# The down stage of an FFN with ScalarE and VectorE in written order: loads of forms three products early, weight sums a unit early

## The chip, the cores and the metric

The kernel runs on one core of one Trainium2 chip. Its engines are TensorE (PE in the profile, its weight loads PEld), VectorE (DVE), ScalarE (ACT), GpSimd (POOL) and SyncE (SP), which issues most of the transfers. The metric is the device time of one execution in microseconds. Each engine works off its own list of instructions in order; semaphores make one engine wait for another.

## The reference

One decoder layer over 512 tokens with 2048 features, float32 in and out. A mixing part (a gated linear recurrence beside RWKV heads) ends in a projection `w_o` with a residual; then comes the feed-forward part that this case is about:

```python
def ffn(h):                       # D_MODEL 2048, D_FF 6144, 512 tokens
    u = rmsnorm(h, ln_ffn)
    g = causal_dwconv(u @ w_gate, conv_f_w, conv_f_b)
    return h + (gelu(g) * (u @ w_up)) @ w_down
```

(in shortened form); after it a gated per-layer embedding and a last norm.

## The kernel before

A float32 product is made from three TensorE products of rounded parts. Each operand is split: ScalarE copies it, rounded, to a high half (`split` L146 for forms of the data, L133 for weights), and VectorE subtracts the high half from the raw value for the low half (L147, L134). Then high times high, high times low and low times high are summed in PSUM (L1382 to L1384 in the down stage, L1274 to L1276 in the gate stage).

Stages that the change touches, in order of time:

- **wo** (L1250 on): for each of 16 feature blocks `m` a product, then VectorE's residual add into `hT[m]` (L1253), then `forms(m)`, which makes from `hT[m]` the block's part of seven operand forms of the next stage (L1241 to L1243, splits L147, L149, L150), then a square for the norm (summed at L1261).
- **gate stage**: gate and up products of the FFN for 48 blocks `n`, each by a Winograd scheme that needs seven units (q5, p1, p4, p6, p7, p2, p3) in place of eight products. A unit takes a weight of 128x1024, which is either loaded as it is or is a sum of quarters of the matrix. `gate_unit` makes these sums, by VectorE (L1127, L1137, L1140) or by an accumulating transfer of GpSimd's queue. `unit` puts the results together; for the last block its closing VectorE addition is L1306 and frees the buffer `e` that it read.
- **down stage**: the hidden features stand in 12 chunks. Chunks 0 to 10 go through a Winograd scheme again, in four groups, seven products for each half `b` of the output:

```python
GROUPS = [(0, 3), (3, 6), (6, 9), (9, 11)]
ORDER = (1, 0, 4, 2, 3, 5, 6)
```

  `down(g, b)` loops over the seven products; each product takes one weight unit of each chunk of its group, and each unit is 12 matmuls of 128x512. The data forms of a group are up to 21 tiles s0 to s20 (tag 3j + chunk within the group, j the product's place in `ORDER`), loaded by the sync queue (L1342) from DRAM and then split; both halves `b` use them, and the next group's forms take the same tiles. Weights of a product 1 or 4 of `ORDER`'s numbers are sums of two quarters by VectorE (`down_unit` L1162, L1168), those of 2 and 6 are accumulated by GpSimd's queue (L1172), 0 and 3 use a quarter that is there, and 5 loads its quarter into one of two buffers `wraw` (L124). A product's result is taken from PSUM by ScalarE in group 0 (L1397) and added by VectorE in the others (L1399). After each half of the last group seven sums (L1407) turn the product sums `PT` into output blocks.
- **the end of the FFN**: `residual`, `down_last` (chunk 11, by plain products of four "last" forms) and `to_features` for four column blocks. `residual` transposes the stored `hT` and adds it (L1427), `down_last` adds its products (L1437).

What sets the order. TensorE's list is in written order. The lists of VectorE, ScalarE and the queues in the stages above are set by a scheduler that simulates the program and takes what is ready by priority; `high_priority(offset=...)` moves an instruction ahead by so many steps. Weights go through a queue: `wqueue` holds the list of all units, and `wnext` hands out the next split unit after `wfill` has prepared ones up to three ahead (`LOOK` 3, and three buffers each of `whi` and `wlo`, so that a unit's high half can be written once TensorE has finished the unit three before). `wfill` makes the raw weight, including its loads and its sum, directly ahead of its split, all with a high priority:

```python
    def wfill(self):
        with self.tc.high_priority(offset=W['offw']):
            self.wfill_()
```

The forms of group g + 1 are loaded and split by one function, called after each product of the half b = 1 of group g; those of group 0 during the units of block 47 of the gate stage.

Of the kernel before, what the change touches and what calls it, by code (L numbers as in the profile page):

```python
# [89 lines left out]
class Builder:  # L90
# [13 lines left out]
    def wqueue(self, items):  # L104
        self.wq = list(items)
        self.wn = 0
        self.wt = []
# [5 lines left out]
    def wfill_(self):  # L113
        nc = self.nc
        while self.wn < len(self.wq) and len(self.wt) < self.LOOK:
            src, shape, *own = self.wq[self.wn]
            self.wn += 1
            if callable(src):
                raw = src()
            elif self.wraw:  # L120
                raw = self.wraw.pop(0)
            else:
                raw = self.t(self.cp, "wraw", shape, bufs=self.RAW)
                nc.sync.dma_start(raw, src)  # L124
# [989 lines left out]
    def gate_unit(self, n, u):  # L1114
# [5 lines left out]
        def load(k, i, j):  # L1120
            t = buf(k)
            nc.sync.dma_start(t, src(i, j))
            return t
        g = self.gw.setdefault(n, {})
        if u == "q5":
            g[21], g[22], g["s"] = load(0, 1, 0), load(1, 1, 1), buf(3)
            nc.vector.tensor_tensor(g["s"], g[21], g[22], ALU.add)  # L1127
            return g["s"]
# [5 lines left out]
        if u == "p7":  # L1134
            if n < 2:
                g[11] = load(2, 0, 0)
            nc.vector.tensor_tensor(g[21], g[21], g[11], ALU.add)  # L1137
            return g[21]
        if u == "p6" and n in (0, NF - 1):
            nc.vector.tensor_tensor(g["s"], g["s"], g[11], ALU.add)  # L1140
        else:
            nc.gpsimd.dma_start(g["s"], src(0, 0 if u == "p6" else 1), accum_op=ALU.add)
# [67 lines left out]
    def phase2(self):  # L1210
# [70 lines left out]
        def unit(n, u):  # L1281
# [29 lines left out]
            if n == NF - 1:  # L1311
                for i in {"q5": (0,), "p1": (1,), "p4": (2, 3), "p6": (4,), "p7": (5,), "p2": (6,)}.get(u, ()):
                    group_form(0, ORDER[i])
# [25 lines left out]
        def hidden(src, tag):  # L1339
            t = T("s%d" % tag, 1, (128, 2, 2, 256), F32R)  # L1340
            r = t[:, 1].bitcast(F32)
            nc.sync.dma_start(r, src)  # L1342
            self.split(t[:, 0], t[:, 1], r)
            return t[:, 0], t[:, 1]

# [5 lines left out]
        def group_form(g, i):  # L1351
            lo, hi = GROUPS[g]
            for ch in range(lo, hi):
# [3 lines left out]
                hids[ch, i] = hidden(src, 3 * ORDER.index(i) + ch - lo)  # L1357
# [28 lines left out]
        def down(g, b):  # L1386
            lo, hi = GROUPS[g]
            for j, i in enumerate(ORDER):
                ps = [self.mm(), self.mm()]
                for ch in range(lo, hi):  # L1390
                    w = self.wnext()
                    for tt in range(2):
                        product(ps[tt], hids[ch, i], w, tt, ch == lo, ch == hi - 1)
# [299 lines left out]
```

## Time and profile before

| | us |
|---|---|
| median of three runs | 2630.39 |
| the three runs | 2632.26, 2629.11, 2630.39 |
| profiled execution | 2625.72 |
| its span (first to last instruction) | 2624.0 |
| mean granted TensorE clock | 0.988 |
| wo to gate | about 902 |
| down stage | about 1883 to 2344 |

The profiled execution is 4.67 us shorter than the median of the runs. In the profile's rows a time in brackets is the idle time of the engine ahead of the instruction, with what ended it. `s<-dd` and `s<-rd` are loads of forms, `x<-wd`, `s<-wd`, `e<-wd` and `wraw<-wd` loads of down weights, numbers of buffers left out. The groups of chunks change at about 1960 to 2040, 2090 to 2165 and 2215 to 2265 us.

### The profile page before, as it was taken

Reading aid. Unit: us, or ns where it says so; the run is one execution under the profiler, and the core shown is the slowest. Engines: PE = TensorE matmul, PEld = TensorE weight load, DVE = VectorE, ACT = ScalarE, POOL = GpSimd, SP = SyncE. Lnnn points to the kernel's source line nnn. Section 1 sums busy time; section 2 is a strip of 40 time slices with the busy share of each in tenths; the row PEclk is TensorE's granted clock in tenths of the full one; section 3 lists DMA queues with packets and bytes.
Section 4 is the critical chain, followed back from the end, with each engine's and each line's share of the span. In section 5 each row is a group of like instructions: output and inputs, shape, how many; then the busy total and the mean of one; then the engine's idle time right before and its main releaser. Section 6 shows DMA issues by size and latency. Waiting matters only on the chain.

```text
span 2624.0 us, 51665 instructions
## 1 busy us (share of the span) xinstructions
PE 2545.0 (97%) x21922; PEld 2241.5 (85%) x21922; DVE 1907.0 (73%) x2603; ACT 1251.5 (48%) x1735; POOL 229.8 (9%) x251
## 2 busy tenths in 40 slices
PE   9989999999999999999999999999999999999997
PEld 8867777777877799999999999999877877787887
DVE  5764875767666978878888888788756777896447
ACT  6563555546433644444444444444545344434335
POOL 0010000101121010000000000000000000000001
PEclk9999999999999999999999999999999999999998
DMA  7222222222343667676677766777767776843223
GB/s 252 93 69 66 87 80 66 86 73 94 94 126 103 222 154 193 177 192 164 191 185 185 188 184 167 193 183 188 220 160 225 189 206 188 233 116 111 96 93 108
DMA packets 131304, 393.76 MB, mean 150 GB/s; under 512 B 14464, under 2 KB 26624, under 8 KB 131072
## 3 DMA queue, kind: packets, MB, share of 16 engines
q1 hardware_dynamic: 111200, 318.10, 35.9%
q0 software_dynamic: 19872, 72.36, 16.7%
q8 instruction: 171, 2.80, 0.4%
q14 instruction: 61, 0.50, 0.1%
HBM read 353.97 MB, written 36.44 MB: 149 GB/s over the span
## 4 chain that ended last, share of the span: by engine, by line
PE 60%; DMA 5%; DVE 4%; ACT 2%; issue 1%; POOL 0%; SPq 0%; POOLq 0%; ACTq 0%; DVEq 0%
PE mm L1275 9%; PE mm L1274 9%; PE mm L1276 9%; PE mm L1383 4%; PE mm L1384 4%; PE mm L1382 4%; PE wk L1274 3%; PE wk L1275 3%; PE wk L1276 3%; PE mm L1488 2%; DMA s<-rd 2%; PE mm L1490 2%; PE mm L1489 2%; DVE wlo L134 2%; PE mm L163 2%; PE mm L165 2%
## 5 line engine op out<-in xcount | busy, mean ns | idle before, releaser
L133 ACT ACTIVATE whi<-x 128x1024 fp32r<-128x1024 f32 x296 | 313.1, 1058 | 410.5 <-PE mm L1275 232.4
L134 DVE TENSOR_TENSOR wlo<-x,whi 128x1024 fp32r<-128x1024 f32 x296 | 361.4, 1222 | 114.0 <-ACT whi L133 107.7
L1274 PE MATMUL mm<-s,whi 128*128 128x256 f32 x1432 | 406.2, 284 | 5.3 <-ACT s L149 4.1
L1275 PE MATMUL mm<-s,whi 128*128 128x256 f32 x1432 | 406.1, 284 | 0.3 <-DVE s L150 0.3
L133 ACT ACTIVATE whi<-wraw 128x1024 fp32r<-128x1024 f32 (+1 forms) x229 | 232.7, 1017 | 363.8 <-PE mm L165 174.3
L1276 PE MATMUL mm<-s,wlo 128*128 128x256 f32 x1432 | 405.9, 283 | 0.0
L134 DVE TENSOR_TENSOR wlo<-wraw,whi 128x1024 fp32r<-128x1024 f32 (+1 forms) x229 | 278.9, 1219 | 157.6 <-ACT whi L133 156.1
L163 PE MATMUL mm<-x,whi 128*128 128x512 f32 x832 | 331.7, 399 | 1.1 <-DVE hT L453 0.9
L167 PE MATMUL mm<-x,wlo 128*128 128x512 f32 x832 | 331.7, 399 | 0.0
L165 PE MATMUL mm<-x,whi 128*128 128x512 f32 x832 | 330.3, 397 | 0.0
L1382 PE MATMUL mm<-whi,s 128*128 128x512 f32 x680 | 269.6, 398 | 14.7 <-ACT whi L133 14.6
L1383 PE MATMUL mm<-wlo,s 128*128 128x512 f32 x680 | 271.3, 399 | 10.6 <-DVE wlo L134 10.0
L1274 PEld LDWEIGHTS mm<-s,whi 128*128 128x128 f32 x1432 | 275.5, 192 | 5.8 <-ACT s L149 4.3
L1275 PEld LDWEIGHTS mm<-s,whi 128*128 128x128 f32 x1432 | 275.6, 192 | 0.6 <-DVE s L150 0.6
L1276 PEld LDWEIGHTS mm<-s,wlo 128*128 128x128 f32 x1432 | 275.6, 192 | 0.0
L1384 PE MATMUL mm<-whi,s 128*128 128x512 f32 x680 | 268.7, 395 | 0.0
L163 PEld LDWEIGHTS mm<-x,whi 128*128 128x128 f32 x832 | 156.8, 188 | 36.8 <-issue 2.9
L167 PEld LDWEIGHTS mm<-x,wlo 128*128 128x128 f32 x832 | 156.8, 188 | 33.8 <-issue 1.9
L165 PEld LDWEIGHTS mm<-x,whi 128*128 128x128 f32 x832 | 156.7, 188 | 33.5 <-issue 1.8
L1383 PEld LDWEIGHTS mm<-wlo,s 128*128 128x128 f32 x680 | 129.8, 191 | 44.9 <-DVE wlo L134 18.4
L1382 PEld LDWEIGHTS mm<-whi,s 128*128 128x128 f32 x680 | 129.5, 191 | 45.1 <-ACT whi L133 18.5
L1274 PE MATMUL wk<-s,whi 128*128 128x256 f32 x584 | 165.7, 284 | 0.0
(572 smaller groups left out, 5497.7 us busy)
## 6 DMA issues: line engine op xcount, KB each, us to landing
x<-wgu SPq DMA_DIRECT2D x144, 512.0 KB, 4.2
x<-wgu POOLq DMA_DIRECT2D x94, 512.0 KB, 5.5
wraw<-wz SPq DMA_DIRECT2D x80, 512.0 KB, 3.5
wraw<-wgu SPq DMA_DIRECT2D x51, 512.0 KB, 4.1
x<-wd SPq DMA_DIRECT2D x34, 512.0 KB, 5.2
x<-wd POOLq DMA_DIRECT2D x32, 512.0 KB, 5.5
wraw<-wpg SPq DMA_DIRECT2D x31, 512.0 KB, 3.5
wraw<-wd SPq DMA_DIRECT2D x30, 512.0 KB, 4.2
```

The source lines that it names most:

```text
L133: nc.scalar.activation(hi, raw, AF.Copy)
L134: nc.vector.tensor_tensor(lo, raw, hi.bitcast(F32), ALU.subtract)
L163: nc.tensor.matmul(ps, hi[:, k, :], xh, start=first and i == 0, stop=False)
L165: nc.tensor.matmul(ps, hi[:, k, :], xl, start=False, stop=False)
L167: nc.tensor.matmul(ps, lo[:, k, :], xh, start=False, stop=last and i == n - 1)
L1274: TE.matmul(ps, wh[:, k, :], xh, start=k == 0, stop=False)
L1275: TE.matmul(ps, wh[:, k, :], xl, start=False, stop=False)
L1276: TE.matmul(ps, wl[:, k, :], xh, start=False, stop=k == 7)
L1382: TE.matmul(ps, x[0][:, k, ts_], w[0][:, k, :], start=first and k == 0, stop=False)
L1383: TE.matmul(ps, x[0][:, k, ts_], w[1][:, k, :], start=False, stop=False)
L1384: TE.matmul(ps, x[1][:, k, ts_], w[0][:, k, :], start=False, stop=last and k == 1)
L1488: TE.matmul(pg[tt], xh[:, ts_], wh[:, i, :], start=first and u + i == 0, stop=False)
```

## The change

Four things:

- **Raw weights ahead.** `wfill_` keeps a list of raw weights and fetches `AHEAD` units further than it splits. `AHEAD` is 0 up to the down stage and 1 from there on, so a unit's loads and sum are written one unit ahead of its split.
- **First sums without priority.** In `gate_unit` the VectorE sums go through a helper `add`, which for the first two blocks takes the priority of `wfill` away again.
- **Loads and splits of forms apart.** Two tables say after how many products a form is loaded and when it is split. A form of group g > 0 is loaded at product 14g - 6 + j and split at product 14g - 4 + j, where 14 products make a group; each chunk's split is written after that chunk's unit. The "last" forms are loaded in the first four products of the last group and split two products later. Of group 0, forms 0, 1 and 2 are loaded after q5, p1 and p4 of block 47, form 0 is split in p4, the rest inside the down stage.
- **Written order.** The whole loop over groups and halves stands in `manual_schedule` for VectorE and ScalarE: their instructions there keep the order in which the code writes them.

```diff
@@ wqueue, wfill_
+        self.raws, self.AHEAD = [], 0
...
         while self.wn < len(self.wq) and len(self.wt) < self.LOOK:
+            while len(self.raws) <= self.AHEAD and self.wn + len(self.raws) < len(self.wq):
+                src, shape = self.wq[self.wn + len(self.raws)][:2]
+                if callable(src):
+                    raw = src()
+                elif self.wraw:
+                    raw = self.wraw.pop(0)
+                else:
+                    raw = self.t(self.cp, "wraw", shape, bufs=self.RAW)
+                    nc.sync.dma_start(raw, src)
+                self.raws.append(raw)
             src, shape, *own = self.wq[self.wn]
+            raw = self.raws.pop(0)
             self.wn += 1
-            if callable(src):
-                raw = src()
...
@@ gate_unit
+        def add(o, a, b):
+            with self.tc.high_priority(offset=-W['offw'] if n < 2 else 0):
+                nc.vector.tensor_tensor(o, a, b, ALU.add)
+            return o
...
-            nc.vector.tensor_tensor(g["s"], g[21], g[22], ALU.add)
-            return g["s"]
+            return add(g["s"], g[21], g[22])
...
@@ unit
             if n == NF - 1:
-                for i in {"q5": (0,), "p1": (1,), "p4": (2, 3), "p6": (4,), "p7": (5,), "p2": (6,)}.get(u, ()):
-                    group_form(0, ORDER[i])
+                if u in ("q5", "p1", "p4"):
+                    load_forms(0, ("q5", "p1", "p4").index(u))
+                if u == "p4":
+                    for ch in range(*GROUPS[0]):
+                        split_form(0, 0, ch)
...
@@ group_form
-        def group_form(g, i):
+        def load_forms(g, j):
...
-                hids[ch, i] = hidden(src, 3 * ORDER.index(i) + ch - lo)
+                hids[ch, i] = load_form(src, 3 * j + ch - lo)
+
+        def split_form(g, j, ch):
+            hi, lo = hids[ch, ORDER[j]]
+            self.split(hi, lo, lo.bitcast(F32))
+
+        loads, splits = {}, {}
+        for g in range(len(GROUPS)):
+            for j in range(7):
+                if g or j > 2:
+                    loads.setdefault(14 * g - 6 + j if g else j - 2, []).append((g, j))
+                if g or j:
+                    splits.setdefault(14 * g - 4 + j if g else j - 1, []).append((g, j))
...
@@ down
+                at = 14 * g + 7 * b + j
+                for f in loads.get(at, ()):
+                    load_forms(*f)
+                if g + 1 == len(GROUPS) and b == 0 and j < 4:
+                    hids["last", j // 2, j % 2] = load_form(quarter(NCH - 1, j // 2, j % 2), 2 + 3 * j)
                 ps = [self.mm(), self.mm()]
                 for ch in range(lo, hi):
                     w = self.wnext()
                     for tt in range(2):
                         product(ps[tt], hids[ch, i], w, tt, ch == lo, ch == hi - 1)
+                    for f in splits.get(at, ()):
+                        for c in range(*GROUPS[f[0]]):
+                            if c - GROUPS[f[0]][0] == ch - lo:
+                                split_form(*f, c)
...
-                if b == 1 and g + 1 < len(GROUPS):
-                    group_form(g + 1, i)
-                if g + 1 == len(GROUPS) and b == 0 and j < 4:
-                    hids["last", j // 2, j % 2] = hidden(quarter(NCH - 1, j // 2, j % 2), 2 + 3 * j)
+                if g + 1 == len(GROUPS) and 2 <= 7 * b + j < 6:
+                    hi_, lo_ = hids["last", (j - 2) // 2, (j - 2) % 2]
+                    self.split(hi_, lo_, lo_.bitcast(F32))
...
-        for g in range(len(GROUPS)):
-            for b in range(2):
-                down(g, b)
+        ET = mybir.EngineType
+        with self.tc.manual_schedule(engines={ET.DVE, ET.Activation}):
+            self.AHEAD = 1
+            for g in range(len(GROUPS)):
+                for b in range(2):
+                    down(g, b)
```

The new lines shift the numbers: the split of weights is L138 and L139 in the changed kernel, that of forms L151 and L152, a form's load L1355, the weight sums of the down stage L1168 and L1174, the gate stage's closing addition L1312, the evictions L1426 and L1428, the final sums L1435, the residual L1458. The order that results, engine by engine, at three places (each row is a line, an operation, output and inputs by the program's names with their numbers, and a size):

ScalarE, second half of group 1, where the first forms of group 2 (s0, s1, ...) come in. Before:

```order
L133 ACTIVATE whi_3147_23271<-e_3130_23201 128x1024
L146 ACTIVATE s0_3153_23321<-s0_3153_23321 128x512
L133 ACTIVATE whi_3149_23287<-e_3135_23223 128x1024
L133 ACTIVATE whi_3151_23303<-x2_3140_23245 128x1024
L146 ACTIVATE s1_3154_23325<-s1_3154_23325 128x512
L146 ACTIVATE s2_3155_23329<-s2_3155_23329 128x512
L133 ACTIVATE whi_3159_23338<-x1_3131_23203 128x1024
L146 ACTIVATE s3_3167_23394<-s3_3167_23394 128x512
L133 ACTIVATE whi_3162_23357<-x5_3136_23225 128x1024
```
and in the changed kernel:

```order
L138 ACTIVATE whi_3176_23433<-s21_3140_23235 128x1024
L138 ACTIVATE whi_3183_23459<-x6_3151_23305 128x1024
L151 ACTIVATE s0_3154_23326<-s0_3154_23326 128x512
L138 ACTIVATE whi_3185_23477<-s23_3159_23334 128x1024
L151 ACTIVATE s1_3155_23328<-s1_3155_23328 128x512
L138 ACTIVATE whi_3188_23497<-e_3162_23353 128x1024
L151 ACTIVATE s2_3156_23330<-s2_3156_23330 128x512
L138 ACTIVATE whi_3196_23527<-wraw_3187_23495 128x1024
L151 ACTIVATE s3_3167_23391<-s3_3167_23391 128x512
```
Before, a form's split stood wherever the scheduler's simulation had its load ready, s1 and s2 on end; now each form's split stands behind the weight split of one unit.

VectorE, end of the gate stage and start of the down stage (x11 and x9 are the last gate results, s3 to s20 forms of group 0). Before:

```order
L134 TENSOR_TENSOR wlo_2918_22011<-s23_2892_21924,whi_2917_22010 128x1024
L1168 TENSOR_TENSOR s22_2893_21926<-s22_2893_21926,x2_2927_22068 128x1024
L134 TENSOR_TENSOR wlo_2923_22034<-x1_2876_21831,whi_2922_22033 128x1024
L147 TENSOR_TENSOR s16_2881_21869<-s16_2881_21869 128x512
L147 TENSOR_TENSOR s17_2882_21873<-s17_2882_21873 128x512
L147 TENSOR_TENSOR s18_2889_21912<-s18_2889_21912 128x512
L147 TENSOR_TENSOR s19_2890_21916<-s19_2890_21916 128x512
L147 TENSOR_TENSOR s20_2891_21920<-s20_2891_21920 128x512
L1306 TENSOR_TENSOR x11_2843_21606<-mm_2883_21877,e_2842_21605 128x512
L1369 TENSOR_TENSOR x11_2843_21606<-x11_2843_21606,x9_2852_21678 128x1024
L1168 TENSOR_TENSOR x5_2885_21880<-x5_2885_21880,e_2924_22049 128x1024
L134 TENSOR_TENSOR wlo_2926_22053<-x5_2885_21880,whi_2925_22052 128x1024
```
and in the changed kernel:

```order
L139 TENSOR_TENSOR wlo_2879_21837<-x3_2877_21834,whi_2878_21836 128x1024
L1309 TENSOR_TENSOR e_2842_21605<-e_2842_21605,wk_2868_21792 128x256
L1310 TENSOR_TENSOR x11_2843_21606<-mm_2844_21607,e_2842_21605 128x512
L1312 TENSOR_TENSOR x11_2843_21606<-mm_2874_21829,e_2842_21605 128x512
L1389 TENSOR_TENSOR x11_2843_21606<-x11_2843_21606,x9_2852_21672 128x1024
L1168 TENSOR_TENSOR s21_2882_21868<-s23_2880_21864,s22_2881_21866 128x1024
L139 TENSOR_TENSOR wlo_2884_21871<-s21_2882_21868,whi_2883_21870 128x1024
L139 TENSOR_TENSOR wlo_2902_21921<-x2_2869_21793,whi_2901_21920 128x1024
L152 TENSOR_TENSOR s3_2856_21712<-s3_2856_21712 128x512
L139 TENSOR_TENSOR wlo_2904_21939<-x6_2875_21830,whi_2903_21938 128x1024
L152 TENSOR_TENSOR s4_2857_21714<-s4_2857_21714 128x512
L1174 TENSOR_TENSOR x1_2870_21795<-x1_2870_21795,e_2905_21956 128x1024
```
The closing addition moved from behind five form splits and two units of down weights to the place right after the last gate unit; the form splits went to between the weight splits.

VectorE, last group, the end of the half b = 0 (before, the rows are those around its fourth to sixth product). Before:

```order
L134 TENSOR_TENSOR wlo_3416_24743<-e_3400_24657,whi_3415_24742 128x1024
L1399 TENSOR_TENSOR x15_2901_21966<-x15_2901_21966,mm_3413_24740 128x512
L1399 TENSOR_TENSOR x15_2901_21966<-x15_2901_21966,mm_3414_24741 128x512
L1407 TENSOR_TENSOR x15_2901_21966<-x15_2901_21966,s27_2897_21962 128x1024
L134 TENSOR_TENSOR wlo_3419_24761<-wraw_3417_24758,whi_3418_24760 128x1024
L1407 TENSOR_TENSOR x8_2899_21964<-x8_2899_21964,x15_2901_21966 128x1024
L134 TENSOR_TENSOR wlo_3425_24787<-wraw_3423_24784,whi_3424_24786 128x1024
L1399 TENSOR_TENSOR x4_2903_21968<-x4_2903_21968,mm_3421_24782 128x512
L1399 TENSOR_TENSOR x4_2903_21968<-x4_2903_21968,mm_3422_24783 128x512
L134 TENSOR_TENSOR wlo_3427_24804<-x0_3378_24546,whi_3426_24803 128x1024
L1407 TENSOR_TENSOR x4_2903_21968<-x4_2903_21968,x8_2899_21964 128x1024
```
and in the changed kernel, after the last product of that half:

```order
L1428 TENSOR_TENSOR x10_2897_21914<-x10_2897_21914,mm_3440_24872 128x512
L1428 TENSOR_TENSOR x10_2897_21914<-x10_2897_21914,mm_3441_24873 128x512
L1435 TENSOR_TENSOR x15_2889_21906<-x15_2889_21906,s27_2885_21902 128x1024
L1435 TENSOR_TENSOR x7_2895_21912<-x7_2895_21912,s27_2885_21902 128x1024
L1435 TENSOR_TENSOR x10_2897_21914<-x10_2897_21914,x12_2893_21910 128x1024
L1435 TENSOR_TENSOR x10_2897_21914<-x10_2897_21914,x15_2889_21906 128x1024
L1435 TENSOR_TENSOR x8_2887_21904<-x8_2887_21904,x15_2889_21906 128x1024
L1458 SCALAR_TENSOR_TENSOR x7_2895_21912<-x7_2895_21912,rsr_1597_11012,wk_3498_25202 128x512
L1435 TENSOR_TENSOR x4_2891_21908<-x4_2891_21908,x8_2887_21904 128x1024
L1435 TENSOR_TENSOR x12_2893_21910<-x8_2887_21904,x12_2893_21910 128x1024
L1174 TENSOR_TENSOR x1_3431_24826<-x1_3431_24826,s23_3448_24917 128x1024
L139 TENSOR_TENSOR wlo_3450_24921<-x6_3435_24846,whi_3449_24920 128x1024
```
The seven final sums, which stood one by one between weight splits, now stand together between the last evictions of the half and the next low half.

From wo to the gate stage on VectorE, the residual add of the last block (m = 15) stood behind five sums of `gate_unit`; in the changed kernel it stands right behind the forms of block 14 and one weight split, and the sums come after it. On the sync queue the order of the down stage's loads is almost the same as before at the changes of group; at the start of the gate stage the stores of two blocks `hd` stand ahead of two weight loads that they followed.

24 lines of the change are left out of this document (8 added, 16 removed).

## The prediction

> **What bounds the kernel now.** I read four views, in this order: the busy time of each engine, windows over the stages that the change touches, the waits of the down stage, and the timeline around the longest of them. The page's first section names the engine:
>
> ```profile
> PE 2545.0 (97%) x21922; PEld 2241.5 (85%) x21922; DVE 1907.0 (73%) x2603; ACT 1251.5 (48%) x1735; POOL 229.8 (9%) x251
> ```
>
> TensorE is busy for 97% of the span, so the change can only win time in which TensorE stands still or runs at a reduced clock. Where that is, the windows tell (start:end, length, busy time and instructions of PE, PEld, DVE, ACT, POOL, granted clock, DMA share, GB/s):
>
> ```profile
> 905.00:910.00 5.00, 5.00 (x44) 5.00 (x43) 5.00 (x8) 2.53 (x4) 0.00 (x0) 1.00 1.03 419
> 910.00:925.00 15.00, 9.39 (x48) 8.60 (x48) 11.98 (x19) 4.45 (x9) 2.52 (x2) 0.66 0.67 221
> 930.00:940.00 10.00, 8.43 (x72) 8.26 (x71) 7.64 (x9) 4.67 (x5) 1.77 (x2) 1.00 0.50 107
> 1885.00:1900.00 15.00, 10.16 (x33) 7.61 (x32) 13.29 (x20) 8.20 (x13) 1.76 (x2) 0.78 0.87 218
> 1900.00:1920.00 20.00, 16.06 (x59) 12.24 (x58) 13.09 (x14) 6.76 (x8) 0.90 (x1) 0.84 0.65 198
> 1960.00:2040.00 80.00, 74.77 (x314) 59.21 (x313) 54.51 (x58) 45.02 (x62) 7.12 (x8) 0.98 0.80 224
> 2090.00:2165.00 75.00, 68.14 (x286) 53.94 (x285) 58.11 (x68) 35.80 (x44) 5.66 (x7) 0.98 0.78 219
> 2165.00:2215.00 50.00, 50.00 (x222) 41.42 (x221) 36.05 (x37) 19.52 (x19) 4.44 (x5) 1.00 0.61 156
> 2215.00:2265.00 50.00, 45.62 (x192) 35.36 (x192) 36.80 (x44) 24.52 (x31) 3.55 (x4) 1.00 0.89 266
> ```
>
> The undisturbed row 2165 to 2215 gives the price of a matmul of the down stage: 50.00/222 = 0.225 us, so a unit of twelve takes 2.70 us. The row 905 to 910 gives 5.00/44 = 0.1136 us for the smaller matmul of the gate stage. Length minus matmuls times that price is what a window lost, by waiting or by a low clock. At the three changes of group: 80 - 314 x 0.2252 = 9.3, 75 - 286 x 0.2252 = 10.6, 50 - 192 x 0.2252 = 6.8, together 26.7 us. At the start of the down stage: 7.6 + 6.7 = 14.3 us. From wo to gate: 15 - 48 x 0.1136 = 9.5 and 10 - 72 x 0.1136 = 1.8, together 11.3 us. These 52 us are all that the change can reach. Who is waited for in the down stage (total, times, longest):
>
> ```profile
> PE mm L1382 <- ACT whi L133: 14.6, 7, 4.8
> PE mm L1383 <- DVE wlo L134: 10.0, 12, 2.0
> ACT s L146 <- DMA s<-dd: 52.7, 22, 4.6
> ACT s L146 <- DMA s<-rd: 44.0, 24, 4.2
> SPq L1342 <- PE mm L1384: 86.4, 27, 14.3
> ```
>
> TensorE waits 24.6 us for split weights, while ScalarE waits 96.7 us for the loads of forms. The last row says when these loads can leave: the sync queue waits until TensorE has finished with the buffer of the old form. One change of group in the timeline shows how the two rows hang together:
>
> ```profile
> 2098.23 0.63 ACT L146 ACTIVATE s<-s 128x512 fp32r<-128x512 f32 x1 [4.10 <-DMA s<-rd]
> 2098.77 1.04 ACT L133 ACTIVATE whi<-x 128x1024 fp32r<-128x1024 f32 x1
> 2099.86 0.51 PE L1382 MATMUL mm<-whi,s 128*128 128x512 f32 x1 [1.13 <-ACT whi L133]
> 2101.38 0.61 PE L1383 MATMUL mm<-wlo,s 128*128 128x512 f32 x1 [1.01 <-DVE wlo L134]
> ```
>
> ScalarE sat 4.10 us before a form's split, whose load had not landed, and the weight split that TensorE needed stood right behind it. The form itself was not needed until the next group. So the cause is the order on ScalarE, not ScalarE's capacity.
>
> **The changes of group.** Loads now stand three products ahead of their splits, where before they stood right ahead of them. Three products are some 9 units x 2.70 = 24 us; the wait for a form was at most 4.6 us. The 96.7 us of ScalarE's waiting should go, and with it TensorE's behind it. What stays: the sixth product takes its three weights unsummed, through two raw buffers, so a third weight's load cannot leave before an earlier split is done:
>
> ```profile
> 2125.09 0.33 SPq L124 DMA_DIRECT2D wraw<-wd  x1
> 2131.28 1.06 ACT L133 ACTIVATE whi<-wraw 128x1024 fp32r<-128x1024 f32 x1 [1.24 <-DMA wraw<-wd]
> ```
>
> That load took 6.2 us, and ScalarE waited 1.24 us for it; the change doesn't add a buffer. Fetching a unit earlier has nothing to fetch into. I charge 1.24 us plus half of one low-clock stretch of 1.6 us (next part), 2.0 us at each of three changes, so 26.7 - 6.0 = 20.7 us are won. Bounds: 26.7 (nothing stays) and 10 (VectorE becomes late, first rival).
>
> VectorE's own budget must hold. Its pitch, from three instructions back to back:
>
> ```profile
> 2331.42 1.22 DVE L1407 TENSOR_TENSOR s<-s,s 128x1024 f32<-128x1024 f32 x1
> 2332.55 1.22 DVE L134 TENSOR_TENSOR wlo<-wraw,whi 128x1024 fp32r<-128x1024 f32 x1
> 2333.69 1.27 DVE L1399 TENSOR_TENSOR x<-x,mm 128x512 f32<-128x512 f32 x2
> ```
>
> A 128x1024 sum or low half takes 1.14 us from start to start, a 128x512 one some 0.60. A product with sums and form splits needs 3 x 1.14 + 3 x 1.14 + 3 x 0.60 + 2 x 0.60 = 9.8 us against 3 x 2.70 = 8.1 us of TensorE, one without sums 6.4. Two products in seven have sums, so a lag of 1.7 us is made up in the next product, and the split runs up to three units (8.1 us) ahead. I cost it at nothing.
>
> **The clock after a wait.** Both long waits at the start, and one pair of short ones, are followed by a low granted clock:
>
> ```profile
> 1894.00:1901.00 7.00, 6.99 (x18) 5.26 (x19) 5.03 (x6) 4.05 (x6) 0.88 (x1) 0.56 0.77 177
> 1914.70:1921.00 6.30, 6.19 (x14) 4.46 (x15) 3.50 (x3) 2.21 (x4) 0.90 (x1) 0.52 0.61 178
> 2098.70:2101.40 2.70, 0.56 (x3) 0.21 (x2) 2.50 (x4) 2.33 (x4) 0.00 (x0) 1.00 0.70 266
> 2101.40:2105.00 3.60, 3.60 (x9) 2.82 (x10) 3.60 (x5) 1.93 (x3) 0.00 (x0) 0.53 0.78 226
> ```
>
> The first lost 6.99 - 18 x 0.2252 = 2.9 us, the second 6.19 - 14 x 0.2252 = 3.0, the last 3.60 - 9 x 0.2252 = 1.6. So a wait of 4 us costs 7, and the pair of 1.13 and 1.01 us cost 1.6 on top. The Trainium skill ("TensorE: Matmul & The Clock Gate", Part 1, "What's actually happening") states that the clock falls to half after an idle window of about 3.4 us and returns after about 3.4 us of work. The two long waits agree, with 0.56 and 0.52; the short pair does not, since it brought 0.53 with a matmul between its waits. By the rule the changes of group would keep 1.24 us each and the gain there would be 23.0 instead of 20.7; I go by the row.
>
> **The start of the down stage.** The rows, in order of time:
>
> ```profile
> 1880.83 1.01 SPq L1154 DMA_DIRECT2D s<-wd  x2
> 1890.98 1.23 DVE L1162 TENSOR_TENSOR s<-s,s 128x1024 f32<-128x1024 f32 x1 [0.48 <-DMA s<-wd]
> 1894.02 1.22 PE L1382 MATMUL mm<-whi,s 128*128 128x512 f32 x2 [4.84 <-ACT whi L133]
> 1904.99 3.09 DVE L147 TENSOR_TENSOR s<-s 128x512 fp32r<-128x512 f32 x5
> 1908.00 0.68 DVE L1306 TENSOR_TENSOR x<-mm,e 128x512 f32<-128x512 f32 x1
> 1908.71 0.33 SPq L1154 DMA_DIRECT2D e<-wd  x1
> 1912.34 1.23 DVE L1168 TENSOR_TENSOR x<-x,e 128x1024 f32<-128x1024 f32 x1 [2.40 <-DMA e<-wd]
> 1914.77 1.22 PE L1382 MATMUL mm<-whi,s 128*128 128x512 f32 x2 [3.90 <-ACT whi L133]
> ```
>
> The first wait (4.84) goes back to two loads issued at 1880.83, which landed 10.1 us later; they keep their place in the sync queue, and I leave it as it is. The second goes back to buffer e: the gate stage's last sum (L1306) frees it, stood behind five form splits until 1908.00, and only then could the load leave that the sum at 1912.34 waits for. In written order that sum (now L1312) follows its product directly, ahead of all down-stage work; the load leaves up to some 20 us sooner. Gain 3.90 + 3.0 = 6.9 us; bounds 0 (another weight takes its place) and 9.9 (part of the first wait goes too).
>
> **From wo to gate.**
>
> ```profile
> 903.89 1.23 DVE L1127 TENSOR_TENSOR x<-x,x 128x1024 f32<-128x1024 f32 x1
> 913.84 0.68 DVE L1253 TENSOR_TENSOR hT<-hT,mm 128x512 f32<-128x512 f32 x1
> 915.12 0.58 PE L1274 MATMUL mm<-s,whi 128*128 128x256 f32 x1 [4.06 <-ACT s L149]
> ```
>
> Between these two VectorE instructions stand five weight sums; the residual add of the last feature block releases everything that the gate stage still needs. Without priority the sums go behind it: it moves from 913.84 to about 907. Of the 11.3 us lost I leave 1.7 (the last forms of that block), 2.2 (the low half of an early unit, now behind three sums: 3 x 1.14 less a 1.2 lead) and the 1.8 of the second window: 5.6 won, taken as 5. Bounds 0 (the sums, now late, stop TensorE instead) and 9.5.
>
> **The last group, between its halves.** Here the change adds. Before, the seven final sums of a half stood one by one between weight splits. In written order all seven come after the half's last eviction, with a residual and a weight sum, ahead of the next low half. From the end of the half's matmuls VectorE needs 2.3 (low half under way, with its wait) + 1.2 (evictions) + 7 x 1.14 = 8.0 + 0.7 + 2 x 1.14 = 14.5 us until that low half is there. TensorE has three split units, 8.1 us, and some 2.0 us of transposes and first-term matmuls: 4.4 us of waiting, with 3 of low clock -7. Bounds -9.5 and 0. The second half has the same lump, but units of 5.4 us behind it: -1 (bounds -3 and +2).
>
> **Sum.** 20.7 + 6.9 + 5 - 7 - 1 = 24.6 us. The profiled execution took 2625.7 us (span 2624.0), 4.7 below the median of the three runs, 2630.4: 2601.1 on its scale, 2605.8 on the median's.
>
> **The rivals.** (A) VectorE becomes the bound: after each lag it is late for several units, since in written order nothing can be drawn ahead. For it speaks 9.8 against 8.1 us; against it, 6.4 in the other products. The changes of group then win 10: 2616, or 2619 with the lump at its bound. (B) The lump is hidden: the scheduler's sequence of loads keeps TensorE fed, or the transposes stretch. Then nothing is lost at the last group: 2598, and 2592 if nothing stays at the changes of group. Against it speaks 14.5 against 10.1. (C) The change doesn't do what it says: the sync queue's order is nearly unmoved, and if TensorE was really waiting for transfers (0.80 to 0.89 of the DMA engines in those windows), the wait moves from the form to the weight. Only start and wo remain: 6.9 + 5 - 8 = 3.9, so 2627, or 2619 with the lump at nothing. (D) Slower: with sums a unit ahead, a sum whose second load is late now stops VectorE before a split that is already due. From a sum's turn to TensorE's need of what is behind it there are some 3 us; its load leaves about 8 us ahead of its turn. It decides at landings above 11 us. The longest seen is 10.1 us, others 3.6 (e) and 6.2. To end 0.2% slower, 24.6 + 5.3 us must be lost over the 22 sums of one kind: 1.4 us each.
>
> **How the numbers follow.** 0.2%, 5.3 us, is about what a measurement can tell from no change. Forecast 0.58 (its own range 2599 to 2613), A 0.15, B 0.11, C 0.10, D 0.06. Faster takes the first three and 0.04 of C: 0.88; same the rest of C, 0.06; slower D. The range 2596 to 2621 holds the forecast, A, the upper part of B and the lower part of C.
>
> **What would show it.** ScalarE's waits for s<-dd and s<-rd near zero; the windows around the three changes of group at 2 us lost each; L1312 ahead of the first form split after form zero, and no wait of 3.9 us near the second sum; the add L1259 of the last block before the first gate sum; one wait of 4 to 5 us with a low clock between the halves of the last group, behind L1435. I'm wrong if the boundaries still show waits for weight splits: then the order was not their cause.

## The result, and the profile after

The changed kernel takes 2613.06 us (median of 4 runs, 2612.49 to 2613.87), the kernel before 2630.51 (4 runs): ratio 0.9934, 95% interval 0.9916 to 0.9951. Run again beside the last experiments it came to 0.9927 (0.9910 to 0.9945). The profiled execution has a span of 2611.5 us, 12.5 less than that of before: 2.4 us were lost ahead of the changed code, and the profiled execution of before was some 5 us below its median.

The same windows as before, of the changed kernel (start:end, length, busy time and instructions of PE, PEld, DVE, ACT, POOL, granted clock, DMA share, GB/s):

```profile
910.00:925.00 15.00, 13.28 (x107) 12.67 (x106) 14.46 (x20) 6.83 (x11) 2.06 (x2) 1.00 0.74 247
930.00:940.00 10.00, 5.06 (x41) 4.66 (x39) 6.53 (x6) 4.95 (x5) 1.81 (x2) 1.00 0.44 105
1885.00:1900.00 15.00, 10.73 (x43) 8.36 (x43) 7.99 (x9) 3.99 (x5) 1.73 (x2) 0.85 1.03 323
1900.00:1920.00 20.00, 20.00 (x84) 16.44 (x83) 14.64 (x16) 13.03 (x19) 0.89 (x1) 0.94 0.72 188
1960.00:2040.00 80.00, 78.92 (x348) 64.80 (x347) 59.87 (x64) 47.51 (x65) 7.89 (x9) 1.00 0.82 236
2090.00:2165.00 75.00, 73.91 (x323) 59.83 (x322) 61.56 (x72) 38.57 (x48) 7.03 (x8) 1.00 0.78 214
2165.00:2215.00 50.00, 47.28 (x201) 38.50 (x200) 33.00 (x33) 17.31 (x17) 3.51 (x4) 0.97 0.69 189
2215.00:2265.00 50.00, 48.35 (x205) 39.30 (x205) 39.69 (x48) 24.57 (x30) 4.39 (x5) 0.97 0.84 244
```

The two windows around the first two changes of group run 348 and 323 matmuls where 314 and 286 ran. The third wins least (205 for 192), and the window ahead of it, which had no loss before, has one now (201 for 222). From wo to gate the first window is far better (107 for 48) and the next worse (41 for 72). The waits of the down stage say who is left (total, times, longest):

```profile
ACT whi L138 <- DMA wraw<-wd: 31.2, 6, 7.9
PE mm L1402 <- ACT whi L138: 10.6, 5, 3.9
PE mm L1403 <- DVE wlo L139: 4.0, 6, 0.8
ACT s L151 <- DMA s<-dd: 2.4, 2, 1.5
```

ScalarE's 96.7 us of waiting for forms are gone. Its 31.2 us now are for raw weights in the two `wraw` buffers.

Since the executions shift against each other, the experiments are read by stages between fixed matmuls (the 10500th to the 11100th, and so on), each profiled execution against that of before. A negative number is time won. The ratio is that of the times to those of the kernel before, run beside each variant:

| run | ratio to before (95%) | wo to gate | start of down | groups 0 to 3 | end of groups, end of FFN |
|---|---|---|---|---|---|
| changed | 0.9934 (0.9916 to 0.9951) | 0.1 | -7.6 | -14.1 | 6.8 |
| changed, again | 0.9927 (0.9910 to 0.9945) | -1.0 | -7.7 | -17.2 | 7.1 |
| gate priority back | 0.9933 (0.9919 to 0.9947) | 0.0 | -9.1 | -20.1 | 6.3 |
| gate weight by VectorE | 0.9912 (0.9894 to 0.9931) | -6.3 | -7.9 | -19.0 | 6.0 |
| tiles exchanged | 0.9906 (0.9884 to 0.9928) | 0.1 | -15.3 | -13.8 | 7.1 |
| not in written order | 0.9978 (0.9964 to 0.9992) | 2.9 | -9.5 | 2.1 | 0.1 |
| sums on time | 1.0005 (0.9994 to 1.0016) | 0.5 | -6.5 | -1.7 | 9.9 |
| neither of the two | 0.9989 (0.9974 to 1.0004) | 1.3 | -8.2 | 2.6 | 0.2 |
| forms split at once | 0.9920 (0.9903 to 0.9937) | -0.6 | -7.8 | -16.9 | 6.7 |
| third weight apart | 0.9905 (0.9888 to 0.9921) | 0.8 | -7.5 | -26.7 | 6.3 |
| final sums spread | 0.9934 (0.9918 to 0.9950) | 2.1 | -9.4 | -15.8 | 4.5 |
| one by one, third apart | 0.9886 (0.9867 to 0.9905) | 1.4 | -8.0 | -26.5 | 3.1 |
| all four edits | 0.9844 (0.9823 to 0.9865) | -3.1 | -15.3 | -26.4 | 4.7 |

A stage figure is one execution against one. In the groups the five runs whose edits don't touch them (changed, changed again, gate priority back, gate weight by VectorE, tiles exchanged) lie between -13.8 and -20.1, so 6 us there are no more than chance; in the first two columns runs whose edits don't touch a stage differ by 3 to 4 us. Several intervals of the ratios overlap with that of the changed kernel. Taken alone, the ratios of the gate weight and of the exchanged tiles are not clear of it; for these two the stage column and the wait itself carry the claim.

### The profile page after: what moved, and what is told of

It is laid out like the page before. It is cut to its first block, busy times and chain, and to the rows that moved or that the text cites. A ratio compares the mean times of both kernels' runs of the same rounds, so it can differ in the third digit from the quotient of the medians.

```text
span 2611.5 us, 51670 instructions
## 1 busy us (share of the span) xinstructions
PE 2543.5 (97%) x21922; PEld 2243.9 (86%) x21922; DVE 1904.5 (73%) x2603; ACT 1249.5 (48%) x1735; POOL 228.2 (9%) x251
## 4 chain that ended last, share of the span: by engine, by line
PE 62%; DVE 5%; DMA 2%; ACT 2%; issue 1%; POOL 0%; ACTq 0%; POOLq 0%; DVEq 0%
PE mm L1282 9%; PE mm L1281 9%; PE mm L1280 9%; PE mm L1403 5%; PE mm L1404 5%; PE mm L1402 5%; PE wk L1281 3%; PE wk L1282 3%; PE wk L1280 3%; PE mm L1519 2%; PE mm L1521 2%; PE mm L1520 2%; PE mm L168 2%; PE mm L170 2%; PE mm L172 1%; DMA wraw<-wd 1%
## 5 line engine op out<-in xcount | busy, mean ns | idle before, releaser
L138 ACT ACTIVATE whi<-x 128x1024 fp32r<-128x1024 f32 x296 | 313.5, 1060 | 441.5 <-PE mm L1281 232.6
L139 DVE TENSOR_TENSOR wlo<-x,whi 128x1024 fp32r<-128x1024 f32 x296 | 361.7, 1223 | 122.6 <-ACT whi L138 116.3
L138 ACT ACTIVATE whi<-wraw 128x1024 fp32r<-128x1024 f32 (+1 forms) x229 | 233.1, 1018 | 382.6 <-PE mm L170 186.4
L139 DVE TENSOR_TENSOR wlo<-wraw,whi 128x1024 fp32r<-128x1024 f32 (+1 forms) x229 | 278.2, 1215 | 176.5 <-ACT whi L138 174.9
L1148 POOL DMA_DIRECT2D x<-wgu x94 | 82.8, 880 | 955.2 <-DVE wlo L139 654.9
L1280 PE MATMUL wk<-s,whi 128*128 128x256 f32 x584 | 165.3, 283 | 0.0
L1281 PE MATMUL wk<-s,whi 128*128 128x256 f32 x584 | 165.3, 283 | 0.0
```

Of the source, the lines that this page charges most:

```text
L138: nc.scalar.activation(hi, raw, AF.Copy)
L139: nc.vector.tensor_tensor(lo, raw, hi.bitcast(F32), ALU.subtract)
L1280: TE.matmul(ps, wh[:, k, :], xh, start=k == 0, stop=False)
L1281: TE.matmul(ps, wh[:, k, :], xl, start=False, stop=False)
```

## The experiments: what wins in the groups

Four variants of the changed kernel take the ingredients apart. The first goes back to the scheduler's order:

```diff
-        with self.tc.manual_schedule(engines={ET.DVE, ET.Activation}):
+        if True:
             self.AHEAD = 1
```

> The loop of the down stage without the written order: ScalarE and VectorE go back to the scheduler, loads and splits stay apart, sums stay a unit ahead. Theory: the order on ScalarE is what wins; if the scheduler still places splits of forms by its own simulated landings, the waits for forms come back in part: 2616 to 2626. Rival: it is the separation of loads and splits alone that wins, so that the written order adds nothing and its lump is the only loss: 2604 to 2610.

Measured 0.9978. The groups lose what they won (2.1 us instead of -14.1), and ScalarE waits for forms as much as in the kernel before, although loads and splits stay apart in the code. Its rows:

```profile
ACT s L151 <- DMA s<-dd: 53.4, 25, 4.2
ACT s L151 <- DMA s<-rd: 45.1, 27, 4.4
```

So the tables of loads and splits alone don't part them: for the forms of groups 1 and 2, paired in order, a split begins 2.5 to 10.5 us after its load is issued, as in the kernel before (2.5 to 9.8), and in the changed kernel 22.5 to 30.0 us after it. The second variant keeps the written order and moves the splits next to their loads:

```diff
-                    splits.setdefault(14 * g - 4 + j if g else j - 1, []).append((g, j))
+                    splits.setdefault(14 * g - 6 + j if g else j - 1, []).append((g, j))
```

> In written order, but a form is split in the product in which it is loaded, two products earlier than in the changed kernel (splits at 14g - 6 + j). Theory: the distance between load and split is what wins, since ScalarE otherwise stands before a form that hasn't landed while TensorE's next weight is queued behind it; then ScalarE's waits for loads of forms come back (some 60 to 100 us in all, 0 to 5 us each) and TensorE loses 8 to 20 us at the three changes of group: ratio to the kernel before 0.997 to 1.001. Rival: the written order and the sums ahead win by themselves and three units of lead cover the landings; then within 3 us of the changed kernel, ratio 0.993 to 0.9945.

Measured 0.9920: nothing is lost, against what I expected. The waits for forms stay away (the one row of them):

```profile
ACT s L151 <- DMA s<-dd: 2.4, 2, 1.6
```

The trace gives the reason. In written order a split stands behind weight splits that are prepared three units ahead, and those wait until TensorE has finished an earlier unit. In this run that puts 7.8 to 14.5 us (mostly 9.1) between the issue of a form's load and its split in groups 1 and 2, while the loads of forms from 1950 to 2130 us took 2.4 to 8.7 us to land. So the written order alone covers the loads, by a narrow margin, and the two products more that the tables give buy nothing here. The third variant takes the sums back to their splits:

```diff
-            self.AHEAD = 1
+            self.AHEAD = 0
```

> The changed kernel with the weight sums directly ahead of their splits again (AHEAD 0). Theory: in written order ScalarE's split then waits for a sum that VectorE has just begun (1.14 us) behind everything else on VectorE; three units of lead cover most of it, so 0 to 6 us are lost, ratio 0.9935 to 0.9957. Rival: a sum a unit ahead stops VectorE for its loads before a split that is due; then without it TensorE gains 2 to 5 us, ratio below 0.9925.

Measured 1.0005: the whole gain is lost, three times what I allowed. The waits for forms don't come back; others take their place:

```profile
ACT whi L138 <- DVE x L1174: 56.7, 15, 13.3
ACT whi L138 <- DVE x L1168: 42.2, 14, 5.0
ACT whi L138 <- DVE s L1168: 24.2, 6, 11.5
ACT whi L138 <- DVE s L1174: 15.3, 6, 2.6
```

ScalarE now waits 138 us for sums, and VectorE, in order, for ScalarE: sum, high half and low half of a unit go one after the other. VectorE at one product with sums (between the low half and the next sum stands a form's split of 0.60 us):

```profile
2009.07 1.22 DVE L1168 TENSOR_TENSOR x<-s,x 128x1024 f32<-128x1024 f32 x1
2011.50 1.23 DVE L139 TENSOR_TENSOR wlo<-x,whi 128x1024 fp32r<-128x1024 f32 x1 [1.21 <-ACT whi L138]
2013.25 1.22 DVE L1168 TENSOR_TENSOR x<-e,x 128x1024 f32<-128x1024 f32 x1
```

and the same place in the changed kernel, where VectorE sums the next unit while ScalarE copies this one:

```profile
2003.47 1.22 DVE L1168 TENSOR_TENSOR x<-s,x 128x1024 f32<-128x1024 f32 x1
2006.34 1.22 DVE L1168 TENSOR_TENSOR x<-e,x 128x1024 f32<-128x1024 f32 x1
```

A unit costs VectorE 4.18 us here and 2.87 us there, where TensorE needs 2.70. From 1860 to 2345 us TensorE waits 11.6 us for low halves (22 times) instead of 4.0 (6 times). Of ScalarE's waits for sums 37 us are left in the changed kernel. The last variant has neither:

> The changed kernel without the written order and with the sums directly ahead of their splits: of the change only the separate loads and splits, and the gate sums without priority, are left. If written order and sums ahead are worth something only together, as the runs with one of them show (0.998 with the sums ahead, 1.0005 with the written order), this one is near them: 0.996 to 1.000, and the three changes of group lose 20 us or more. Rival: each is worth its part by itself, so that this one is slower than both: above 1.003.

Measured 0.9989, groups 2.6. Only the start of the stage is won (8.2 us), and it is won without the written order: the closing addition L1312 runs at 1891.53 and the load into `e` leaves at 1892.30, where the kernel before had 1908.00 and 1908.71. With scheduler or written order, and sums on time or ahead, the four ratios are 0.9989, 0.9978, 1.0005 and 0.9934: neither ingredient wins in the groups by itself, both together do. (TensorE's list, too, is the scheduler's in these stages, which the description of the kernel has too simply. Against the changed kernel it differs at 224 of 21922 places in the two runs without written order and at 454 in the one with sums on time, where first matmuls of a unit change places. What that is worth by itself no run tests.)

## The experiments: what the change left, and what it gave back

**The third weight.** Of the sixth product's three weights the last waits for a `wraw` buffer. The rows of the changed kernel where it was worst, ScalarE's split and TensorE's two waits, and then windows over three such places, each with the stretch behind it:

```profile
2173.47 1.06 ACT L138 ACTIVATE whi<-wraw 128x1024 fp32r<-128x1024 f32 x1 [7.91 <-DMA wraw<-wd]
2174.57 0.50 PE L1402 MATMUL mm<-whi,s 128*128 128x512 f32 x1 [1.96 <-ACT whi L138]
2175.84 0.80 PE L1403 MATMUL mm<-wlo,s 128*128 128x512 f32 x1 [0.76 <-DVE wlo L139]
```

```profile
2172.60:2176.00 3.40, 0.68 (x3) 0.35 (x3) 1.44 (x2) 2.53 (x3) 0.00 (x0) 0.93 0.03 13
2176.00:2179.40 3.40, 3.40 (x9) 2.72 (x10) 3.40 (x5) 0.42 (x1) 0.00 (x0) 0.57 0.51 154
2234.40:2236.70 2.30, 0.66 (x3) 0.25 (x2) 1.34 (x2) 2.30 (x4) 0.00 (x0) 1.00 0.41 167
2236.70:2240.10 3.40, 3.40 (x9) 2.71 (x10) 3.40 (x5) 1.56 (x3) 0.00 (x0) 0.54 0.71 218
1997.20:1998.90 1.70, 0.62 (x3) 0.26 (x2) 1.35 (x2) 1.70 (x5) 0.00 (x0) 1.00 0.32 122
1998.90:2002.30 3.40, 3.40 (x15) 2.82 (x16) 2.79 (x4) 3.40 (x6) 0.00 (x0) 1.00 0.65 213
```

The load left at 2164.12 and was there 9.2 us later. Two of the three places are followed by a low clock, nine matmuls in 3.4 us instead of fifteen. The edit loads the third weight into the rotation of the plain buffers:

```diff
+        if i == 5:
+            return plain(1, 0)
...
-                        if i == 5:
+                        if i == 5 and ch - lo < 2:
```

> The third weight of the sixth product is loaded into a buffer of the plain slots instead of waiting for one of the two wraw buffers. Theory: the waits of TensorE at 1997, 2114, 2174 and 2235 us (6.2 us in all, some low clock behind the longest) come from that buffer, so they go: 7 to 9 us less, about 2605. Rival: the transfers are slow there for traffic (9.3 us from issue to landing at 2164); then a longer lead moves the wait elsewhere, and less than 3 us are won.

Measured 0.9905, and in the groups -26.7 us, as much as the prediction had read as lost there. No wait of TensorE is left between the start of the stage and the halves of the last group. So a load that is issued earlier removes the wait. That this load took 9.2 us, where loads into `wraw` between 1885 and 2270 us took 3.4 to 9.2, had its part in it, and what made it slow isn't shown.

**The lump of final sums.** VectorE and TensorE at the halves of the last group, changed kernel:

```profile
2290.82 2.35 DVE L1435 TENSOR_TENSOR x<-x,s 128x1024 f32<-128x1024 f32 x2
2293.09 3.62 DVE L1435 TENSOR_TENSOR x<-x,x 128x1024 f32<-128x1024 f32 x3
2296.62 0.74 DVE L1458 SCALAR_TENSOR_TENSOR x<-x,rsr,wk 128x512 f32<-128x512 f32 x1
2297.28 2.35 DVE L1435 TENSOR_TENSOR x<-x,x 128x1024 f32<-128x1024 f32 x2
2299.55 1.22 DVE L1174 TENSOR_TENSOR x<-x,s 128x1024 f32<-128x1024 f32 x1
2301.99 0.79 PE L1402 MATMUL mm<-whi,s 128*128 128x512 f32 x1 [3.92 <-ACT whi L138]
```

The wait for the high half comes from the weight sum (L1174) behind the seven. The first edit writes each sum after the product that completes its inputs, and the last product takes PT[4] + PT[2], made ahead, as one sum:

```diff
+        FINAL = {3: ((2, 2, 0, ALU.add), (1, 1, 2, ALU.subtract)), 4: ((3, 3, 1, ALU.add),),
+                 5: ((5, 5, 0, ALU.add), (0, 4, 2, ALU.add), (4, 1, 4, ALU.subtract)), 6: ((6, 6, 0, ALU.add),)}
...
```

> The seven final sums of a half of the last group are written as soon as their inputs are there (two after the fourth product, one after the fifth, three after the sixth, one at the end; the last product takes the sum of two others instead of two sums). If the lump of sums ahead of a low half makes the wait between the halves of the last group, that wait (3.92 us) and the low clock behind it go: about 7 us less than the changed kernel, 2606. Rival: TensorE waits there for a transfer or for the residual's transposes; then the wait stays at 3 to 4 us and the time at 2612 to 2613.

Measured 0.9934, no gain that can be told apart. The trace says why. Of 3.92 us the wait falls to 1.61, since three sums and a residual addition still stand together ahead of the last low halves, and the low clock stays:

```profile
2288.69 1.23 DVE L1436 TENSOR_TENSOR s<-x,x 128x1024 f32<-128x1024 f32 x1
2289.92 0.75 DVE L1459 SCALAR_TENSOR_TENSOR x<-x,rsr,wk 128x512 f32<-128x512 f32 x1
2290.59 1.22 DVE L1436 TENSOR_TENSOR x<-x,x 128x1024 f32<-128x1024 f32 x1
2292.99 0.79 PE L1403 MATMUL mm<-wlo,s 128*128 128x512 f32 x1 [1.61 <-DVE wlo L139]
```

The next variant writes one sum behind each unit or product (2 + 0; 1 - 2; 2 + 4; 3 + 1; 1 - 4; 5 + 0; 6 + 2), together with the third weight apart:

> The third weight of the sixth product in a plain buffer, and the seven final sums one by one, each behind a unit or the last evictions of its product. Theory: the buffer is worth 7 to 9 us as by itself; of the lump's 7.0 us the two left (2.1 us in the first variant, where three sums stood together behind the sixth product) go down to those of the residual, so 4 to 6 us more: ratio 0.988 to 0.989, between the halves of the last group a wait below 1 us and no low clock. Rival: what is left there is the residual's additions and transposes; then 2 us more than the buffer alone, ratio 0.990.

Measured 0.9886, against 0.9905 with the third weight alone; the two intervals overlap. The end of the groups costs 3.1 us instead of 6.8, and the longest wait at the halves is 0.70 us at full clock:

```profile
2290.93 0.50 PE L1404 MATMUL mm<-whi,s 128*128 128x512 f32 x1 [0.70 <-ACT whi L138]
```

**From wo to gate.** First the priority alone is given back (`offset=0` in `add`).

> The first sums of the gate stage get their priority back, all else as changed. In the traces the change won 7 us at 920 us and gave all of it back by 945 us. Theory: the part is worth nothing, because two accumulating transfers, one after the other, set when the gate stage gets going; so within 2 us of the changed kernel, 2611 to 2615. Rival: the part is worth the 5 us that were forecast and the profiled execution was unlucky; then 2618.

Measured 0.9933, the same: that part of the change is worth nothing. In the changed kernel TensorE stood 7 us ahead at 930 us and had lost it by 947. The rows, GpSimd's accumulating transfers, ScalarE's splits and TensorE:

```profile
922.93 1.08 POOL L1148 DMA_DIRECT2D x<-wgu  x1 [92.41 <-DVE rsm L199]
930.29 2.00 ACT L138 ACTIVATE whi<-x 128x1024 fp32r<-128x1024 f32 x2 [5.70 <-DMA x<-wgu]
930.53 0.95 POOL L1148 DMA_DIRECT2D x<-wgu  x1 [5.43 <-issue]
935.88 1.06 ACT L138 ACTIVATE whi<-x 128x1024 fp32r<-128x1024 f32 x1 [3.59 <-DMA x<-wgu]
940.95 2.05 PE L210 MATMUL wk<-con,rsr 128*128 128x128 f32 x8 [5.15 <-DVE e L1306]
```

In the kernel before, the same steps stand at nearly the same times:

```profile
930.07 2.01 ACT L133 ACTIVATE whi<-x 128x1024 fp32r<-128x1024 f32 x2 [2.21 <-DMA x<-wgu]
930.25 0.90 POOL L1142 DMA_DIRECT2D x<-wgu  x1 [4.87 <-issue]
935.78 1.06 ACT L133 ACTIVATE whi<-x 128x1024 fp32r<-128x1024 f32 x1 [3.70 <-DMA x<-wgu]
```

The second accumulating transfer leaves 0.2 us after the split of the first one's weight could begin, in both kernels; why it waits so long, the profile doesn't name ("issue"). What VectorE owes TensorE at 940.95 is queued behind that weight's low half. TensorE waits 5.15 us there where the kernel before waited 1.57, and the granted clock is 0.50 from 939.92 to 946.75, where it was 1.00 before; together that is the 7 us. To break the chain, block 1's p6 is summed by VectorE from a plain load:

```diff
-            if n < 2:
+            if n == 0:
                 g[11] = load(2, 0, 0)
...
+        if u == "p6" and n == 1:
+            g[11] = load(2, 0, 0)
-        if u == "p6" and n in (0, NF - 1):
+        if u == "p6" and n in (0, 1, NF - 1):
```

> The changed kernel with one of the first two accumulated weights of the gate stage (block 1, p6) summed by VectorE from a load of the sync queue. Theory: the two accumulating transfers, of which the second leaves only when the first has landed (930.5 us after 930.3), set when the gate stage gets going, and the 7 us that the sums without priority win are given back there; then 4 to 7 us are won, ratio 0.9908 to 0.992. Rival: the sync queue's loads are what is late (one more of them here); then nothing or a loss, ratio 0.9934 or more.

Measured 0.9912, and 6.3 us won in this stage. TensorE's wait for the same step falls from 5.15 to 2.42, and no low clock follows:

```profile
936.48 1.13 PE L210 MATMUL wk<-con,rsr 128*128 128x128 f32 x8 [2.42 <-DVE e L1308]
```

Whether this edit would win as much with the priority given back wasn't run.

**The first wait of the stage.** The tiles of two operand forms are exchanged, so that two quarters can be loaded earlier:

```diff
-        KIND = ("q5", "p1", "p4", "p6", "p7", "p2", "p3")
+        KIND = ("q5", "p1", "p4", "p2", "p7", "p6", "p3")
```

> The changed kernel with the tiles of two gate forms exchanged (p6 and p2), so that the buffers of the third unit's two quarters come free two gate units earlier and their loads stand some nine loads earlier in the sync queue. Theory: the first wait of the down stage (3.5 us and 0.8 us, with some 3 us of low clock behind) is for these loads, which leave at 1882.6 us and land 10.1 us later among the loads of forms; then 4 to 7 us less, ratio 0.991 to 0.9925 where the changed kernel has 0.9934. Rival: the transfers of forms take the traffic at that time whatever the order; then the wait passes to the next weight and less than 2 us are won.

Measured 0.9906; the start wins 15.3 us instead of 7.6, about all that the prediction read as lost there (14.3). The window has no wait and no low clock:

```profile
1885.00:1900.00 15.00, 15.00 (x68) 12.39 (x67) 13.76 (x15) 10.29 (x15) 1.73 (x2) 1.00 1.06 342
```

**All four.** One by one, third weight apart, gate weight by VectorE, tiles exchanged:

> All four edits together: third weight in a plain buffer (7 to 12 us), final sums one by one (4 to 6), block 1's p6 summed by VectorE (4 to 7), the exchange of tiles (4 to 7). If they touch separate waits, they add up: 19 to 30 us less than the changed kernel, ratio 0.982 to 0.986. Rival: TensorE waits for transfers, and what one wait gives the next takes; then no more than the two that were measured together, 0.988.

Measured 0.9844 (0.9823 to 0.9865): the median is 2588.61 us where the kernel before has 2630.04 in the same comparison. Against 0.9934, the pair of third weight and sums wins 0.0048 by itself, the gate weight 0.0022 and the tiles 0.0028, together 0.0098; all four win 0.0090, or 0.0083 against the changed kernel beside them (0.9927). So the gains add up for the most part. The gate stage keeps 3.1 of its 6.3 us in this execution, with a wait of 2.98 us and 3.4 us of low clock at the same step. The engines' busy time:

```profile
PE 2536.9 (98%) x21922; PEld 2241.6 (87%) x21922; DVE 1907.4 (74%) x2604; ACT 1251.1 (48%) x1735; POOL 227.6 (9%) x250
```

And the changed kernel beside them:

> The changed kernel once more, beside the others on this chip: 0.9934 as before, within 0.0016.

Measured 0.9927, within what was expected.

## Why the prediction was right or wrong

The time, 2613 us, lies within the range of 2596 to 2621, 7 us above the forecast and at the edge of its own range. The sum was 24.6 us and the medians differ by 17.5. No error made up for another: two of the five terms were too high, and the time lies inside because the range was wide enough to hold rival (A) too. By steps:

- **Start of the down stage** (6.9): 7.6 measured. The second wait is gone because L1312 frees `e` in time, the first stays (3.51 us), as the prediction had it. The reason given was the written order, and it isn't needed: the two runs without it win 8.2 and 9.5 us here. What they keep is that most forms of group 0 are loaded and split inside the down stage, no longer ahead of L1312. The rows of the changed kernel, for those at 1908.00 and 1908.71 before:

```profile
1886.23 0.69 DVE L1312 TENSOR_TENSOR x<-mm,e 128x512 f32<-128x512 f32 x1 [1.50 <-PE mm L1282]
1886.99 0.33 SPq L1160 DMA_DIRECT2D e<-wd  x1
```

- **Changes of group** (20.7): 14.1 and 17.2 in two executions. The cause was right: the waits for forms held up weight splits on ScalarE. The reason given for their going was wrong. I put it down to the three products between load and split, and the run with splits at once shows that these buy nothing; the written order removes the waits, and it wins only with sums a unit ahead, which I costed at nothing in either direction and whose absence costs the whole gain. The step on VectorE's budget counted its work (9.8 against 8.1 us for a product) and not the chain through ScalarE (4.18 against 2.70 us a unit without sums ahead).
- **The third weight** (2.0 at three places, 6.0): it is the rest of the miss. At the price of 0.2252 us a matmul the three windows at the changes of group now lose 1.6, 2.3 and 3.8 us, near the 2.0 each that were forecast; but the window from 2165 to 2215, which lost nothing before, loses 4.7. The wait comes in each half of groups 0 to 2, thus six times, also away from the changes of group, and one load took 9.2 us instead of 6.2. What the change left in the groups was 26.7 - 14.1 = 12.6 us in the first execution and 9.5 in the second, and it went with the buffer; by the ratios the buffer is worth 6 to 8 us.
- **From wo to gate** (5): 0 measured. The step that failed is "the low half of an early unit, now behind three sums", which I took for the next limit: TensorE did gain 7 us there and gave it back to a chain of two accumulating transfers and the low clock behind that wait. The bound of 0 was in the range, its mechanism was not named.
- **The last group's halves and the end** (-7 and -1): -6.8 and -7.1 together. The wait was 0.64 + 3.92 us against 4.4, with the low clock behind it.

The rival that VectorE becomes late (2616) had nearly the right time for another reason; VectorE's own work held TensorE up only at the lump. The slower rival, a late load that stops VectorE behind a sum a unit ahead, did not occur in the groups: sums a unit ahead are what wins there, together with the order. VectorE waited for a sum's load once, 4.49 us at 1892.74, which is the first wait of the stage.

## What to carry to other kernels

When two in-order engines hand work to each other (sum, copy, difference), a fixed order needs the producer's step written one item ahead; here the same fixed order without it gave nothing (1.0005 against 0.9934). After a wait is removed, look up who held the next one: here two buffers for three loads, seven sums in a row, and a pair of transfers in a chain kept some 4 to 8 us each, and each was cut by one small edit. A gain at one point of the bounding engine counts only if it is still there some 20 us later.

## What the runs showed of the hardware

Two waits of the kernel before that no low clock followed:

```profile
2132.39 0.50 PE L1382 MATMUL mm<-whi,s 128*128 128x512 f32 x1 [1.72 <-ACT whi L133]
2133.65 0.50 PE L1383 MATMUL mm<-wlo,s 128*128 128x512 f32 x1 [0.76 <-DVE wlo L134]
```

Waits of the same size do not cost the same. Waits of 0.89 and 0.76 us were followed by 3.4 us at half clock at 2236.7, waits of 0.33 and 0.76 at 1997 by none; in the kernel before, 1.72 and 0.76 us at 2132 were followed by none and 1.13 and 1.01 at 2099 by a low clock of 0.53. The low stretches in the traces, those at the two ends of an execution apart, are 3.4 us long or multiples of it. The Trainium skill ("TensorE: Matmul & The Clock Gate", Part 1, "What's actually happening") has the clock fall after an idle window of about 3.4 us. That length agrees; that less idle time than that is enough, with matmuls in it, is what the rule does not say and these rows show.

The traces also tell the cases apart. Within each execution the low stretches begin at whole multiples of 3.413 us from each other. Cut on that grid, from about 1885 to 2410 us, the 14 profiled executions give 2109 cells at full clock (a matmul counts as 0.226 us of work from its start, the rest of a cell as idle). All 43 cells that a low clock followed had 1.90 us or more of idle time. Of the others only one did (2.00 us); the next had 1.87. The waits at 2099 and 2236.7 left 2.59 and 2.20 us idle in one cell. Those at 2132 were cut by the edge of a cell into 1.83 and 1.24 us, those at 1997 into 0.75 and 0.92. So what a short wait costs here depends on where it falls on the grid, and the grid lies differently in each execution. That 1.9 us is the limit in any other kernel is not shown.
